# A hybrid mLSTM and gated-delta encoder block: smaller inversion chunks beside the products, and the next z job's first split moved ahead of the last pair's final step

## The chip, the cores and the metric

The kernel runs on one core of a Trainium2 chip. The metric is the device time of one execution in microseconds (us). Engines are named as in the profile: PE is TensorE (PEld its weight loads), DVE is VectorE, ACT is ScalarE, POOL is GpSimd, SP is SyncE. SPq, ACTq and POOLq are the DMA issues of these engines.

## The reference

One encoder layer on 256 tokens of width 2048, in float32. Cut to what matters here:

```python
h = rms_norm(x) * (1 + scale_m) + shift_m          # scale, shift, gate from silu(c) @ W_ada
proj = h @ w_in                                    # 18,512 columns, split into the branches
# branch A: bidirectional chunkwise mLSTM, 4 heads, q/k 256 wide, v and output gate 512 wide
# branch B: bidirectional gated delta rule, 16 heads of 128:
a_mat = I + beta * (k k^T) * decay_strict          # per chunk of 64 tokens, unit lower triangular
t_mat = triangular_solve(a_mat, I)                 # its inverse
u = t_mat @ (beta * v);  w = t_mat @ (beta * exp(g) * k)
# ... scan over the chunks; o_b = rms_norm(o) * silu(z)
x = x + gate_m * ((g_a * y_a + g_b * y_b) @ w_out)
x = x + gate_f * swiglu(rms_norm(x) * (1 + scale_f) + shift_f)
return rms_norm(x)
```

## The kernel before

Every large product is computed in three passes of 32-bit matmuls: the weights are loaded as float32 (`raw`), ACT writes their rounded high half (`wh`, L182 or L213), DVE subtracts it for the low half (`wl`, L184 or L215), and PE adds hi*hi, lo*hi and hi*lo (L187 to L189, L234 to L236). `raw`, `wh` and `wl` have three buffers each, shared by all jobs.

Two generators make the products. `fjob` makes 128 columns of `w_in` for all 256 tokens: two steps of one split and 24 matmuls of 256 columns. `tjob` makes 512 columns: eight steps of one split and twelve matmuls of 512 columns. One step of either is called a unit here. Such jobs, which nothing waits for soon, stand in the list `fills`: z of a group of delta-rule heads, v and the output gates of the mLSTM heads, the merge gates (`ma`, `mb`), and q and k of the mLSTM heads (`a`). `fill(n)` takes n units from the front of the list, and does nothing once the list is empty. The list is one fixed order, `[z0] + rest`, and each later z job is put at its front when its group comes up.

The delta rule goes in four groups `g` of four heads. A group's life is this:

- `gdn_phase1(h)` (two steps for each head) makes the decay matrices, the key products (`ks`) and the 32 by 32 diagonal blocks `mi`, which POOL writes to DRAM (`inst_d`) and reads back as `uu`. Its second step ends on DVE with the transpose of L657.
- `gdn_invert(g)` inverts the 64 blocks of a group at once, on DVE alone: 30 rounds of two operations (L704, L710) with i from 30 down to 1, on i times 31-i elements. A running size of the rounds stops it every so often (`yield`), and `invert(g)` issues one unit of products at each stop. Before the first round it issues four units (six for group 0). The result goes back to DRAM (`inv_d`).
- `gdn_blocks(g)` reads the blocks, transposes and spreads them; eight units and one unit are issued beside it.
- `gdn_phase2(g, p)` finishes the heads in two pairs p, in nine steps: `p1` to `p4` build the inverse of 128 by 128, `pa`, `pb`, `pc` apply it, `po` makes the output and starts its norm, and the ninth step transposes the normalised output (`px`, L841), copies it (`obt`, L845) and stores it to DRAM (`ob_d`).

Around the nine steps of a pair, `stream` hands out pieces: the products of the next two heads (`b` jobs) with their `gdn_phase1` steps, then units of `fills`. How many pieces follow each step stands in three tuples, for pair 0, pair 1 and group 3:

```python
    after = (0, 1, 2, 1, 2, 2, 2, 2, 4, 0)
    last = (0, 1, 2, 1, 2, 2, 1, 1, 3, 0)
    second = (0, 2, 2, 1, 2, 2, 2, 2, 3, 0)
```

For groups 0 to 2, the sixteenth and last piece of pair 1, behind step 8, carries the second `gdn_phase1` step of the last head of the next group. `heads[h]` are what that step leaves.

Behind group 3 the mLSTM heads 0 and 1 go on (`pden`, then `ph`), the pool `sx` of the delta rule is closed, the outputs of all groups are loaded (`o4`, L1076) and split (`obh` and `obl`, L1080 and L1081), and the products `yb` read them. `fill(1)`, `fill(2)` and `fill(1000)` stand in between and issue what is left of the list.

The program text is not the order on the engines. A planner (the tile framework's scheduler) orders each engine's instructions by when it expects them to be ready, and by their place in the text where several are. `order(ins)` restricts it: the instruction is kept behind the one issued just before it in the text on the same engine. In `tjob` it is used for the splits if `early` is not 0:

```python
            order(S.activation(wh, raws[u][:, k0 : k0 + 2], AF.Copy), early)
            settle()
            order(V.tensor_tensor(wl, raws[u][:, k0 : k0 + 2], wh.bitcast(F32), ALU.subtract), early)
```

`early` is also the number of splits that a job makes before its first matmul; the job then stops once. `settle()` issues what earlier steps have put off, among it the copies of the blocks' corners by ACT (L679, L682). A z job has `early=0` before, except the first (3). `pump()` in each unit moves on the sums of the modulation (`ada`, L124), which run beside the products.

Of the kernel before, what the change touches and what calls it, by code (L numbers as in the profile page):

```python
# [52 lines left out]
def hybrid_block(ctx: ExitStack, tc: tile.TileContext, xr, nfr, crow, pk_d, cst_d, ada2, ada4, win0, winb, wint, wba, wbb, wo, wgu, wd, out, dbg=None):  # L53
# [3 lines left out]
    def pool(stack, name, bufs=1, **kw):  # L57
        return stack.enter_context(tc.tile_pool(name=name, bufs=bufs, **kw))
# [13 lines left out]
    def order(ins, yes=True):  # L72

        return tc.keep_in_program_order(ins) if yes else ins
# [64 lines left out]
    def settle(keep=0, only=None):  # L139

        now = [f for f in behind if only is None or f.__name__ == only]
        for f in now[: len(now) - keep]:
            behind.remove(f)
            f()
# [122 lines left out]
    fills = []  # L267

    def fill(n=1):

        while n and fills:
            if next(fills[0], None):
                n -= 1
            else:
                fills.pop(0)
# [90 lines left out]
    def z_job(g, early=0):  # L366
        def done(ps):
            szs[g] = evp.tile([P, 2, 512], F32, tag="sz", bufs=1, name=f"sz{g}")
            for t in range(2):
                S.activation(szs[g][:, t], ps[t], AF.Silu)  # L370
        return tjob(f"z{g}", [wint[g, u] for u in range(4)], hh, hl, done, early)
# [121 lines left out]
    with ExitStack() as s0:  # L493
# [72 lines left out]
        zj = z_job(0, 3)  # L566
# [121 lines left out]
    def gdn_invert(g):  # L688

        uu = uus.pop(g)  # L690
        tmp = bk.tile([64, 256], F32, tag="utmp", bufs=1, name=f"utmp{g}")
        inv = inv_d[g].rearrange("j b (x h) i -> h (b x) j i", h=GRP)

        def store(rows):
            for e in range(GRP):
                G.dma_start(inv[e, :, rows], uu[16 * e : 16 * e + 16, rows])

        yield
        order(V.memset(uu.rearrange("p j i -> p (j i)")[:, ::33], 1.0))
        size = 0  # L700
        for i in range(30, 0, -1):
            w = 31 - i
            t3 = tmp[:, 0 : i * w].rearrange("p (j c) -> p j c", j=i)
            order(V.tensor_tensor(  # L704
                t3,
                uu[:, 0:i, i : i + 1].broadcast_to([64, i, w]),
                uu[:, i : i + 1, i + 1 :].broadcast_to([64, i, w]),
                ALU.mult,
            ))
            order(V.tensor_tensor(uu[:, 0:i, i + 1 :], uu[:, 0:i, i + 1 :], t3, ALU.add))  # L710
            if i == 16:
                store(slice(16, 32))
            size += i * w + 125
            if size > 720:
                size = 0
                yield
        store(slice(0, 16))

    def gdn_blocks(g):

        cg = bk.tile([P, 2, 512], F32, tag="uu", bufs=1, name=f"cg{g}")
        for b in range(4):
            G.dma_start(cg[32 * b : 32 * b + 32, 0], inv_d[g][:, b].rearrange("j x i -> j (x i)"))
        yield
        order(V.transpose(cg[:, 1], cg[:, 0]))
        F_, Bt, Ft, B_ = (cg[:, i // 2, (i % 2) * 256 : (i % 2 + 1) * 256].rearrange("p (m c) -> p m c", m=8) for i in range(4))

        def mix(dst, a, ca, b, cb):
            order(V.tensor_scalar(dst, b, cb, None, ALU.mult))
            order(V.scalar_tensor_tensor(dst, a, ca, dst, ALU.mult, ALU.add))  # L730

        mix(R[:, 0], Ft, even, Bt, odd)
        mix(R[:, 1], B_, even, F_, odd)
        yield
        for i, ab in enumerate(((Ft, Bt), (B_, F_))):
            for b in range(4):
                r = slice(32 * b, 32 * b + 32)
                order(S.activation(X[r, i, :, b % 2], ab[b // 2][r], AF.Copy))
            yield
        for i, a in enumerate((F_, B_)):  # L740
            for b in range(4):
                r = slice(32 * b, 32 * b + 32)
                if i:
                    order(V.tensor_copy(UL[r, i, :, r], a[r]))
                else:
                    order(S.activation(UL[r, i, :, r], a[r], AF.Copy))
            yield
# [139 lines left out]
    def stream(h0):  # L887

        todo = []

        def piece():

            for q in list(todo):
                q[0] -= 1
                if not q[0]:
                    todo.remove(q)
                    next(heads1[q[1]])

        for h in range(h0, min(h0 + 2, NH_B)):
            for j in range(3):  # L900
                for _ in b_job(h, j):
                    piece()
                    yield True
            todo += [[2, h], [4, h]]
        while todo:
            fill(1)
            piece()
            yield True
        while True:
            fill(1)  # L910
            yield True
# [106 lines left out]
    def invert(g):  # L1018
        gen = gdn_invert(g)
        next(gen)  # L1020
        fill(4 if g else 6)
        for _ in gen:
            fill(1)

    invert(0)
    for g in range(4):
        blocks = gdn_blocks(g)
        next(blocks)
        fill(8)
        next(blocks)  # L1030
        fill(1)
        pairs = [gdn_phase2(g, p) for p in range(2)]
        if g == 3:
            settle()
            sf.close()
            mq["pool"] = pool(sq_, "mq", side="right")
            first2 = [mlstm(h) for h in range(2)]
            for c in first2:
                next(c)
        every[0] = 1  # L1040
        for p in range(2):
            pieces = stream(4 * g + 2 * p + 4)
            for n in range(1, 10):

                held[0] = n < 4
                if p == 0:
                    next(blocks, None)
                next(pairs[p], None)
                if g == 3 and n == (8, 4)[p]:
                    next(first2[p])  # L1050
                for _ in range(last[n] if g == 3 else second[n] if p else after[n]):
                    next(pieces)
            for _ in pairs[p]:
                pass

            if g < 3:
                while 4 * g + 2 * p + 5 not in heads:
                    next(pieces)
        if g < 3:
            fills.insert(0, z_job(g + 1))  # L1060
            every[0] = owed[0] = 0
            invert(g + 1)
    settle()
# [499 lines left out]
```

## Time and profile before

| | us |
|---|---|
| median of 3 runs | 1973.03 (1969.95 to 1974.28) |
| the profiled execution | 1974.3 |
| its span, first to last instruction | 1972.4 |
| PE busy | 1929.4 |
| DVE busy | 1405.5 |
| ACT busy | 1030.0 |
| mean granted clock of PE | 0.994 |

The profile is of one execution. A row of a timeline gives the start, the duration, the engine, the line of the kernel, the operation, output and inputs by the program's names, and in brackets the idle time before it with what ended it. A row of a list of waits gives who waited for whom: total, number of times, longest. A row of a group gives count, busy time, mean ns of one, and idle time before. PE's matmuls are pipelined, so their durations overlap; the distance of two starts tells what one costs.

### The profile page before, as it was taken

To read this page: it belongs to the slowest core of one execution; us is meant where nothing else is said; L and a number is where in the kernel's file an instruction comes from. 1 tells how busy PE (TensorE), PEld (TensorE's weight loads), DVE (VectorE), ACT (ScalarE), POOL (GpSimd) and SP (SyncE) were. 2 spreads that over 40 slices of the span, in tenths; PEclk is the share of its full clock that TensorE was granted. 3 is DMA by queue.
4 is the path that set the end of the run, shared out by engine and by line. 5 is a ranking of instruction groups with operands and counts; after the bars stand their busy time and mean duration, and the time that the engine had idled before them with its cause. 6 is when DMAs were issued, how large, how long until landed. Compare 5 with 4: busy or idle time off the path is not lost.

```text
span 1972.4 us, 27079 instructions
## 1 busy us (share of the span) xinstructions
PE 1929.4 (98%) x10418; PEld 1703.5 (86%) x10418; DVE 1405.5 (71%) x2067; ACT 1030.0 (52%) x1555; POOL 116.5 (6%) x211
## 2 busy tenths in 40 slices
PE   8999999999999999999999999999999999999998
PEld 6878889998998899889787888888888888888886
DVE  6779887887888798866577878866665665555554
ACT  3137656764766577565544444644444444444444
POOL 0001210111001010110100000200000000000000
PEclk9999999999999999999999999999999999999999
DMA  9987676766566666586777888566676665565663
GB/s 399 420 349 226 184 249 240 252 214 208 203 217 213 237 218 229 192 296 246 277 282 266 323 317 330 191 252 238 238 265 241 237 238 205 197 213 197 208 199 142
DMA packets 78962, 485.64 MB, mean 246 GB/s; under 512 B 10585, under 2 KB 15969, under 8 KB 24433
## 3 DMA queue, kind: packets, MB, share of 16 engines
q1 hardware_dynamic: 63216, 450.69, 62.9%
q0 software_dynamic: 8160, 17.88, 4.5%
q10 hardware_dynamic: 7458, 15.36, 2.1%
q8 instruction: 81, 1.33, 0.3%
q14 instruction: 47, 0.39, 0.1%
HBM read 467.07 MB, written 16.82 MB: 245 GB/s over the span
## 4 chain that ended last, share of the span: by engine, by line
PE 81%; DVE 8%; DMA 6%; ACT 2%; issue 1%; POOL 0%; ACTq 0%; SPq 0%; DVEq 0%; POOLq 0%
PE acc_gt L234 4%; PE acc_gt L235 4%; PE acc_gt L236 4%; PE acc_up L236 4%; PE acc_up L235 4%; PE acc_up L234 4%; PE acc_d L236 4%; PE acc_d L235 4%; PE acc_d L234 4%; DMA ra<-ada 3%; PE acc_b L187 2%; PE acc_b L188 2%; PE acc_b L189 2%; PE acc_o L236 2%; PE acc_o L234 2%; PE acc_o L235 2%
## 5 line engine op out<-in xcount | busy, mean ns | idle before, releaser
L215 DVE TENSOR_TENSOR wl_d<-raw_d,wh_d 128x1024 fp32r<-128x1024 f32 x88 | 107.7, 1224 | 105.9 <-ACT wh_d L213 105.9
L215 DVE TENSOR_TENSOR wl_up<-raw_up,wh_up 128x1024 fp32r<-128x1024 f32 x88 | 107.7, 1224 | 100.2 <-ACT wh_up L213 100.1
L215 DVE TENSOR_TENSOR wl_gt<-raw_gt,wh_gt 128x1024 fp32r<-128x1024 f32 x88 | 108.1, 1229 | 80.2 <-ACT wh_gt L213 80.2
L187 PE MATMUL acc_b<-hh,wh_b 128*128 128x256 f32 x576 | 163.0, 283 | 0.6 <-ACT wh_b L182 0.6
L189 PE MATMUL acc_b<-hh,wl_b 128*128 128x256 f32 x576 | 159.6, 277 | 0.8 <-DVE wl_b L184 0.8
L188 PE MATMUL acc_b<-hl,wh_b 128*128 128x256 f32 x576 | 159.2, 276 | 0.0
L213 ACT ACTIVATE wh_d<-raw_d 128x1024 fp32r<-128x1024 f32 x88 | 92.9, 1056 | 126.5 <-PE acc_d L235 117.7
L213 ACT ACTIVATE wh_gt<-raw_gt 128x1024 fp32r<-128x1024 f32 x88 | 92.9, 1056 | 118.6 <-PE acc_gt L235 71.1
L213 ACT ACTIVATE wh_up<-raw_up 128x1024 fp32r<-128x1024 f32 x88 | 92.8, 1055 | 108.1 <-PE acc_up L235 77.1
L124 DVE SCALAR_TENSOR_TENSOR ada<-ada,crow 128x2048 f32<-128x2048 f32 x64 | 146.0, 2284 | 0.0
L234 PE MATMUL acc_gt<-wh_gt,hfh 128*128 128x512 f32 x352 | 135.6, 385 | 0.6 <-ACT hfh L1350 0.6
L235 PE MATMUL acc_gt<-wh_gt,hfl 128*128 128x512 f32 x352 | 134.9, 383 | 0.0
L236 PE MATMUL acc_gt<-wl_gt,hfh 128*128 128x512 f32 x352 | 134.1, 381 | 0.0
L234 PE MATMUL acc_up<-wh_up,hfh 128*128 128x512 f32 x352 | 133.4, 379 | 0.0
L235 PE MATMUL acc_up<-wh_up,hfl 128*128 128x512 f32 x352 | 133.4, 379 | 0.0
L236 PE MATMUL acc_up<-wl_up,hfh 128*128 128x512 f32 x352 | 133.4, 379 | 0.0
L234 PE MATMUL acc_d<-wh_d,ffh 128*128 128x512 f32 x344 | 130.5, 379 | 0.0
L235 PE MATMUL acc_d<-wh_d,ffl 128*128 128x512 f32 x344 | 130.5, 379 | 0.0
L236 PE MATMUL acc_d<-wl_d,ffh 128*128 128x512 f32 x344 | 130.4, 379 | 0.0
L561 PE MATMUL first<-x,raw 128*128 128x256 f32 x512 | 114.5, 382 | 7.2 <-ACT x L555 7.2
L561 PEld LDWEIGHTS first<-x,raw 128*128 128x128 f32 x512 | 96.0, 190 | 25.7 <-ACT x L555 13.3
L189 PEld LDWEIGHTS acc_b<-hh,wl_b 128*128 128x128 f32 x576 | 111.3, 193 | 1.0 <-DVE wl_b L184 1.0
(383 smaller groups left out, 5263.1 us busy)
## 6 DMA issues: line engine op xcount, KB each, us to landing
ada<-ada SPq DMA_DIRECT2D x64, 1024.0 KB, 6.0
raw_gt<-wgu SPq DMA_DIRECT2D x44, 1024.0 KB, 4.9
raw_up<-wgu SPq DMA_DIRECT2D x44, 1024.0 KB, 4.9
raw_d<-wd SPq DMA_DIRECT2D x44, 1024.0 KB, 4.9
raw_b<-winb SPq DMA_DIRECT2D x36, 1024.0 KB, 5.3
ra<-ada SPq DMA_DIRECT2D x32, 1025.0 KB, 15.8
raw<-win SPq DMA_DIRECT2D x16, 1024.0 KB, 14.5
raw_z<-wint SPq DMA_DIRECT2D x16, 1024.0 KB, 5.0
```

The lines of the kernel that those rows point to most:

```text
L124: order(V.scalar_tensor_tensor(raw, raw, 1.0, row_c[:, :D], ALU.mult, ALU.mult, accum_out=mod[:, c : c + 1]))
L187: PE.matmul(o, wh[:, k], woven(hh[:, kk]), start=kk == 0, stop=False)
L188: PE.matmul(o, wh[:, k], woven(hl[:, kk]), start=False, stop=False)
L189: PE.matmul(o, wl[:, k], woven(hh[:, kk]), start=False, stop=kk == KB - 1)
L213: order(S.activation(wh, raws[u][:, k0 : k0 + 2], AF.Copy), early)
L215: order(V.tensor_tensor(wl, raws[u][:, k0 : k0 + 2], wh.bitcast(F32), ALU.subtract), early)
L234: order(PE.matmul(ps[t], xh[:, kk, c], woven(wh[:, k]), start=kk == 0, stop=False), early and steps > 1)
L235: PE.matmul(ps[t], xl[:, kk, c], woven(wh[:, k]), start=False, stop=False)
L236: PE.matmul(ps[t], xh[:, kk, c], woven(wl[:, k]), start=False, stop=kk == last)
L561: PE.matmul(first[o], raw[:, o], x[:, b], start=b == 0 and o % 2 == 0, stop=b == KB - 1 and o % 2 == 1)
```

## The change

Two things. The limit at which `gdn_invert` stops goes from 720 to 580. And the z job of the next group is made with `early=1` and started at n = 9 of pair 1, ahead of the pair's ninth step; its remaining units go to the front of the list where the whole job went before.

```diff
@@ -711,7 +711,7 @@
                 store(slice(16, 32))
             size += i * w + 125
-            if size > 720:
+            if size > 580:
                 size = 0
                 yield
@@ -1045,6 +1045,9 @@
                 if p == 0:
                     next(blocks, None)
+                if g < 3 and p and n == 9:
+                    zj = z_job(g + 1, 1)
+                    next(zj)
                 next(pairs[p], None)
@@ -1057,7 +1060,7 @@
         if g < 3:
-            fills.insert(0, z_job(g + 1))
+            fills.insert(0, zj)
             every[0] = owed[0] = 0
             invert(g + 1)
```

## The prediction

> **What bounds the kernel now.** I read the page's totals first, then the chain that ended last, then who TensorE waited for, and only then the timelines around the places the diff touches.
>
> ```profile
> span 1972.4 us, 27079 instructions
> ...
> PE 1929.4 (98%) x10418; PEld 1703.5 (86%) x10418; DVE 1405.5 (71%) x2067; ACT 1030.0 (52%) x1555; POOL 116.5 (6%) x211
> ...
> PE 81%; DVE 8%; DMA 6%; ACT 2%; issue 1%; POOL 0%; ACTq 0%; SPq 0%; DVEq 0%; POOLq 0%
> ```
>
> TensorE (PE) is the bound over the whole span. The diff neither adds nor removes a matmul, so it can only move time in which PE stands still. The list of PE's waits has those that lie near the change:
>
> ```profile
> PE acc_z L234 <- ACT wh_z L213: 2.5, 1, 2.5
> PE acc_mb L236 <- DVE wl_mb L215: 1.8, 2, 1.0
> PE acc_ma L236 <- DVE wl_ma L215: 1.6, 2, 0.9
> PE acc_a L189 <- DVE wl_a L184: 0.2, 1, 0.2
> ```
>
> ```profile
> PE acc_mb L236 <- DVE wl_mb L215: 1.0, 1, 1.0
> PE acc_o L236 <- DVE wl_o L215: 0.8, 1, 0.8
> ```
>
> The second fence is the same list for the stretch from 435 to 480 us, the inversion of group 1. Each column is the total, the number of times and the longest. With one more pair in group 2 and a short one in group 3, PE loses 1.8 + 1.6 + 0.8 + 0.2 = 4.4 us to low splits (`wl`) that DVE delivers late, and 2.5 us where the z job of group 3 begins. These 6.9 us, with what the clock adds to the second (below), are the most that the change can win.
>
> **Part 1: smaller chunks.** VectorE (DVE) in the inversion stretch of group 1:
>
> ```profile
> L704 DVE TENSOR_TENSOR utmp<-uu 64x30 f32<-64x30 f32 (+14 forms) x30 | 9.7, 322 | 2.2 <-DMA uu<-inst_d 1.4
> L710 DVE TENSOR_TENSOR uu<-uu,utmp 64x30 f32<-64x30 f32 (+14 forms) x30 | 9.7, 322 | 0.8
> L215 DVE TENSOR_TENSOR wl_o<-raw_o,wh_o 128x1024 fp32r<-128x1024 f32 x7 | 8.5, 1209 | 0.0
> ```
>
> One inversion is 60 operations of 322 ns, 19.3 us, and one low split is 1.21 us. The loop's own size sums to 8,710 over the 30 rounds; at a limit of 720 it stops 10 times, at 580 it stops 12 times (and one round is left for after the last stop). At each stop `fill(1)` issues one unit of products: one split and twelve 512-column matmuls (or 24 of 256 columns), which PE starts 0.215 us apart:
>
> ```profile
> 429.88 0.38 PE L235 MATMUL acc_z<-wh_z,hl 128*128 128x512 f32 x1
> 430.09 0.38 PE L236 MATMUL acc_z<-wl_z,hh 128*128 128x512 f32 x1
> 430.31 0.38 PE L234 MATMUL acc_z<-wh_z,hh 128*128 128x512 f32 x1
> ```
>
> So a unit is 12 x 0.215 = 2.58 us of PE. The largest chunk now (rounds 20 to 18, size 1,057) is 1,057 / 8,710 x 19.3 = 2.34 us, and with its split 3.55 us: PE falls 0.97 us behind, which is the size of the waits above. After the change the largest (823) gives 1.82 + 1.21 = 3.03 us and the usual one (712) 1.58 + 1.21 = 2.79 us, still a little over 2.58 but without the jumps. By itself this part wins at most the 4.4 us, and at least nothing.
>
> It also takes 2 units more in each of four inversions, 8 units or 20.6 us of PE work, from a list with an end. I count the list: z jobs 4 x 8, the four v jobs 32, the merge, gate and k/q jobs 26 + 3 x 32: 186 units. Now 19 go in the gates, 18 in the first four heads, 6 + 10 + 3 x (4 + 10) = 58 in the inversions, 36 at the blocks, 24 in the pairs of groups 0 to 2 and 26 in those of group 3: 181, and the five that remain stand in the `fill(1)`, `fill(2)` and `fill(1000)` behind the last pair. With 66 in the inversions the list is empty three calls before the end of the last pair, and those eight calls issue nothing. What they issue now is in PE's groups from the end of `po` of the last pair (938.6) to the first matmul of `yb` (972.6):
>
> ```profile
> L234 PE MATMUL acc_ma<-wh_ma,hh 128*128 128x512 f32 x32 | 12.8, 399 | 0.0
> L235 PE MATMUL acc_ma<-wh_ma,hl 128*128 128x512 f32 x32 | 12.1, 379 | 0.0
> L236 PE MATMUL acc_ma<-wl_ma,hh 128*128 128x512 f32 x32 | 12.1, 379 | 0.0
> L978 PE MATMUL ph<-vt,mdec 128*128 128x512 f32 x24 | 10.5, 592 | 0.0
> L962 PE MATMUL pden<-ones,mdec 128*128 128x1 f32 x24 | 2.7, 247 | 0.0
> L841 PE MATMUL px<-cst,on 128*128 128x128 f32 x4 | 0.6, 272 | 0.0
> ```
>
> 96 `acc_ma` matmuls are exactly eight units. Without them 10.5 + 2.7 + 0.6 = 13.8 us of PE work are left to cover the way from `po` to `yb`. That way is a chain:
>
> ```profile
> 938.22 0.39 PE L834 MATMUL po<-z,at 128*128 128x128 f32 x2
> ```
>
> ```profile
> 941.84 1.13 DVE L868 SCALAR_TENSOR_TENSOR on<-po,so,sz 128x128 f32<-128x128 f32 x4
> ```
>
> ```profile
> 947.17 0.82 ACT L845 ACTIVATE obt<-px,pk 128x256 f32<-128x256 f32 x2
> ...
> 958.72 1.06 ACT L1080 ACTIVATE obh<-o 128x1024 fp32r<-128x1024 f32 x1 [3.16 <-DMA o<-ob_d]
> ```
>
> ```profile
> 951.18 1.51 POOL L1076 DMA_DIRECT2D o<-ob_d  x2 [57.51 <-ACT dn L964]
> ```
>
> ```profile
> 959.81 1.22 DVE L1081 TENSOR_TENSOR obl<-o,obh 128x1024 fp32r<-128x1024 f32 x1 [2.99 <-ACT obh L1080]
> ```
>
> `po` ends at 938.61 and the normalised heads are ready at 942.97, 4.4 us later. The transposes (0.6 us) could follow; now they sit behind three units. From the start of `obt` (947.17) over its store, the release of the group's pool (all of `sx`, so POOL issues the `o` loads only at 951.18), the load and the split, `obl` is there at 961.03: 13.9 us. With no units in between `obt` starts at about 942.97 + 0.6 + 0.35 = 943.9 (0.35 is my estimate for the step from PE to ACT) and `obl` stands at 957.8, that is 19.2 us behind the end of `po`. PE then idles 19.2 - 13.8 = 5.4 us. Lower bound: 2.4 us, if the load, which takes 7.5 us here, lands 3 us sooner in a quieter moment. Upper bound: 10.6 us, if the second half of `ph` (about 5.2 us) also waits, because its PSUM banks are drained by ACT, whose queue would then hold `obh` ahead. I take 5.4.
>
> **Part 2: the z job ahead.** With `early=1` every split of this job goes through `order`, which pins it behind the instruction issued before it on its engine. That matters more than the place of the call. At n = 9 the last thing issued on DVE is the second step of the pair's last head, ending in the transpose of L657. Today z's low splits are free and the planner puts them well ahead of it:
>
> ```profile
> 424.53 1.22 DVE L215 TENSOR_TENSOR wl_z<-raw_z,wh_z 128x1024 fp32r<-128x1024 f32 x1
> ...
> 431.27 0.43 DVE L657 STREAM_TRANSPOSE mi<-mb 128x256 f32<-128x256 f32 x1
> ...
> 438.50 1.23 DVE L215 TENSOR_TENSOR wl_z<-raw_z,wh_z 128x1024 fp32r<-128x1024 f32 x1 [1.22 <-ACT wh_z L213]
> 441.15 0.19 DVE L704 TENSOR_TENSOR utmp<-uu 64x30 f32<-64x30 f32 x1 [1.42 <-DMA uu<-inst_d]
> ```
>
> Pinned, the first `wl_z` of group 1 starts at 431.70 and ends at 432.9, and the first L236 moves from 430.09 to there: 2.8 us of PE. Nothing else is in reach: `ks` and `px` are done, and later units need the same three split buffers. Group 2 has the same picture:
>
> ```profile
> 613.50 0.38 PE L236 MATMUL acc_z<-wl_z,hh 128*128 128x512 f32 x1
> ```
>
> ```profile
> 614.68 0.43 DVE L657 STREAM_TRANSPOSE mi<-mb 128x256 f32<-128x256 f32 x1
> ```
>
> 615.11 + 1.2 = 616.3 against 613.50, again 2.8 us. The pins also hold z's fifth split behind the first chunk, its sixth behind the second, and so on, while today six are done (the first and the last of them stand above) when the inversion starts (at 441.15, when `uu` lands, which the change doesn't move). For the first 16 units of group 1 (4 ahead, 12 at the stops) DVE then needs until 441.15 + 19.3 - 0.3 + 12 x 1.21 = 474.7, and PE ends 2.58 us later, at 477.2; now PE begins z at 429.6, two matmuls ahead of that L236, and the same 16 end at 429.6 + 16 x 2.58 + 1.8 = 472.7. So +4.5 us if DVE sets the pace throughout, +1.0 (2.8 less the 1.8 of part 1) if the later, unpinned splits slip ahead of the chunks as they do now. DVE is full there, so I take the upper half: 3.5 us each for groups 1 and 2, in which part 1's gain is already spent.
>
> Group 3 is the place where the step helps:
>
> ```profile
> 790.30 0.60 PE L841 MATMUL px<-cst,on 128*128 128x128 f32 x4
> 793.41 0.79 PE L234 MATMUL acc_z<-wh_z,hh 128*128 128x512 f32 x1 [2.51 <-ACT wh_z L213]
> ...
> 794.67 0.79 PE L236 MATMUL acc_z<-wl_z,hh 128*128 128x512 f32 x1
> ```
>
> ```profile
> 792.36 0.43 DVE L657 STREAM_TRANSPOSE mi<-mb 128x256 f32<-128x256 f32 x1
> 793.39 1.23 DVE L215 TENSOR_TENSOR wl_z<-raw_z,wh_z 128x1024 fp32r<-128x1024 f32 x1 [0.60 <-ACT wh_z L213]
> ```
>
> The high split can move ahead of `obt`, but the low one still stands behind L657: 792.79 + 1.23 = 794.02 instead of 794.62. I take -0.6 us; if both came in time it would be -2.5 us and what the clock costs. The moved call issues one load on SP, one ACT and one DVE instruction; the load was issued early before, POOL gets nothing new, and the two `obt` copies behind the ACT split are read only by their store.
>
> After this wait PE runs slow for a while; the row is that of the windows, PEclk behind the five busy times:
>
> ```profile
> 793.28:796.69 3.41, 3.24 (x7) 2.15 (x8) 1.86 (x2) 3.33 (x9) 1.97 (x4) 0.50 0.11 19
> ```
>
> Half the clock for 3.41 us costs 1.7 us, and a wait of 2.5 us was enough. I add 1.7 us once, for the idle time of 5.4 us at the end of group 3, and none for the waits of 2.8 us in groups 1 and 2, where DVE sets the pace behind them; 3.4 us for those two go into the upper bound. The Trainium skill, "TensorE: Matmul & The Clock Gate", Part 1, says that the clock is halved after at least one idle window of about 3.4 us, free-running: by that rule the 2.8 us waits would cost no clock at all, and the 3.4 us would leave my upper bound; the row, where 2.5 us sufficed, speaks against relying on it.
>
> **Sum.** +3.5 +3.5 -0.6 +5.4 +1.7 = +13.5 us. The profiled execution took 1974.3 us (span 1972.4 and 1.9 around it) and would become 1987.8; the median of the three runs is 1.3 us lower, so 1973.0 + 13.5 = 1986.5. One `ada` step fewer is done before group 3 ends and returns in the `o` products, where DVE is ahead of PE; I cost it at nothing, and at 2.3 us (one `ada` operation) if it isn't hidden.
>
> **Rivals.** *Faster.* The point that decides is whether the planner still gets z's first low split out before PE needs it (an earlier `ks`, hence an earlier L657) and whether the end of group 3 is cheap. For it: the planner already brings z's splits forward in groups 1 and 2. Against it: L657 hangs on `ks`, which PE runs just before `px`. If both hold: -4.4 - 2.5 - 1.7 + 2.4 = -6.2 us, 1966.8. *Even:* the waits go (-8.6) and the end costs its 5.4 + 1.7: -1.5 us, 1971.5; with one of the two handovers late it is +1.3, 1974.3. *The end is covered:* the planner draws `pden` and `ph` so far forward that only the handovers count: 3.5 + 3.5 - 0.6 + 1 = +7.4, 1980.4. *Worse:* `ph` stalls behind `obh` and both handovers pay for the clock: 13.5 + 5.2 + 3.4 = +22.1, 1995.1.
>
> **How the numbers follow.** 0.2% (3.9 us) is about what a measurement of this kernel can tell from no change. Forecast 0.50 (its own range 1982 to 1992), covered end 0.17, worse 0.10, even 0.11, faster 0.12. The first three are all slower by over 0.2%: 0.77. The even case gives 0.10 for within 0.2% and its rest goes to faster: 0.13. The range leaves out the faster case and the top of the worse one: 1973 to 1994.
>
> **What would show it.** Of the changed kernel: the waits of `acc_z` L236 on `wl_z` in groups 1 and 2, near 2.8 us each, and the first `wl_z` right behind L657 in all three handovers; twelve stops in the inversions and no wait of 0.9 us in their middle; no `acc_ma` matmul between the last `po` and `yb`, and PE idle there for 5 us, with the clock at 0.50 behind it. I am wrong if `wl_z` still stands ahead of L657, or if PE finds other products behind the last `po`.

## The result, and the profile after

| | before | after |
|---|---|---|
| median, us | 1972.8 (1968.5 to 1974.4, 6 runs) | 1986.93 (1984.4 to 1990.8, 6 runs) |
| ratio | | 1.0077, 95% interval 1.0060 to 1.0094 |
| span of the profiled execution, us | 1972.4 | 1986.4 |

The changed kernel is 14.1 us slower by the medians and 15.2 us by the ratio (the ratio is of means); the forecast was 1986.5. The page after, totals and chain:

```profile
span 1986.4 us, 27089 instructions
...
PE 1935.6 (97%) x10418; PEld 1709.4 (86%) x10418; DVE 1405.3 (71%) x2067; ACT 1025.5 (52%) x1551; POOL 116.9 (6%) x211
...
PE 83%; DVE 6%; DMA 6%; ACT 2%; issue 2%; POOL 0%; SPq 0%; ACTq 0%; DVEq 0%; POOLq 0%
```

PE still sets the time, with as many matmuls (10418). PE's list of waits over the whole span (total, times, longest):

```profile
PE acc_z L236 <- DVE wl_z L215: 14.1, 7, 4.9
PE first L561 <- ACT x L555: 6.9, 15, 1.7
PE px L841 <- DVE on L868: 3.6, 1, 3.6
...
PE acc_o L236 <- DVE wl_o L215: 2.4, 2, 2.1
...
PE p L770 <- DVE pt L762: 1.2, 1, 1.2
```

The waits for the low splits of `ma` and `mb`, the 0.9 us ones in the middle of the inversions, are gone, and the one wait for z's high split too. In their place PE waits 14.1 us for z's low split. In group 2's handover the timelines of PE and DVE show how:

```profile
622.38 0.60 PE L841 MATMUL px<-cst,on 128*128 128x128 f32 x4
...
623.47 0.38 PE L235 MATMUL acc_z<-wh_z,hl 128*128 128x512 f32 x1
626.02 1.12 PE L236 MATMUL acc_z<-wl_z,hh 128*128 128x512 f32 x2 [2.18 <-DVE wl_z L215]
```

```profile
624.43 0.43 DVE L657 STREAM_TRANSPOSE mi<-mb 128x256 f32<-128x256 f32 x1
624.79 1.18 DVE L215 TENSOR_TENSOR wl_z<-raw_z,wh_z 128x1024 fp32r<-128x1024 f32 x1
```

The first low split stands right behind L657, as the pin demands. From the L235 at 623.47 to the L236 at 626.02 are 2.55 us where 0.215 would do: 2.34 us lost, and the same 2.34 us in groups 1 and 3. The waits of PE that the text names are taken in this way, from start to start; they come out some 0.16 us longer than the idle time in the lists.

The clock behind the waits, in the view of stretches (the first number behind the five busy times is the granted clock):

```profile
439.90:443.30 3.40, 3.19 (x15) 2.82 (x16) 3.40 (x6) 2.84 (x3) 1.67 (x4) 1.00 0.30 46
626.16:629.57 3.41, 3.41 (x9) 2.66 (x10) 3.41 (x5) 1.70 (x3) 2.19 (x4) 0.50 0.33 43
643.23:646.64 3.41, 3.41 (x10) 2.69 (x9) 3.20 (x9) 0.00 (x0) 0.00 (x0) 0.50 0.00 0
820.72:824.13 3.41, 3.41 (x9) 2.69 (x10) 2.36 (x2) 1.74 (x3) 1.14 (x3) 0.50 0.36 58
380.40:383.81 3.41, 3.41 (x18) 3.41 (x17) 3.41 (x7) 2.23 (x8) 1.67 (x4) 0.50 0.48 130
970.91:981.15 10.24, 8.60 (x32) 6.97 (x33) 2.09 (x13) 2.55 (x7) 1.35 (x2) 0.50 0.15 46
```

Of three equal waits of 2.34 us two were followed by 3.41 us at half clock (rows 2 and 4), the one in group 1 was not (row 1). Row 3 lies behind a longer wait inside group 2's inversion, row 5 behind a wait of 1.34 us of `p` for `pt` in group 0 (1.2 in the list). The last row is the end of group 3, whose PE groups from the last `po` to `yb` are:

```profile
L978 PE MATMUL ph<-vt,mdec 128*128 128x512 f32 x24 | 12.0, 661 | 0.0
L962 PE MATMUL pden<-ones,mdec 128*128 128x1 f32 x24 | 5.1, 334 | 0.0
L841 PE MATMUL px<-cst,on 128*128 128x128 f32 x4 | 1.6, 462 | 3.6 <-DVE on L868 3.6
L234 PE MATMUL acc_yb<-wh_yb,obh 128*128 128x512 f32 x1 | 0.8, 780 | 0.0
```

No `acc_ma` is left there; PE stands for 3.6 us until the norm (`on`) is ready, and of the 17.1 us from there to `yb` (972.55 to 989.67) it spends 8.6 at half clock.

**Where the time went.** From the starts of all PE instructions I take, for each stage, the time beyond 0.2155 us for a 512-column matmul and 0.108 us for a narrower one, and subtract the same of the kernel before. "z1" is the first matmul of z of group 1, "p1" the first of a group's `p1`. Half clock counts in it. us, one profile each:

| stage | after | e1 | e2 | e3 | e5 | e6 | e7 | e8 | e9 | e10 | e12 |
|---|---|---|---|---|---|---|---|---|---|---|---|
| p1 g0 to z1 | 3.1 | 4.6 | 0.0 | 3.1 | 1.5 | 2.9 | 0.0 | 0.0 | 1.5 | 4.6 | 0.0 |
| z1 to p1 g1 | 2.1 | -0.4 | 2.9 | -1.0 | 1.9 | 2.0 | 2.5 | 0.1 | 2.2 | -0.9 | 0.1 |
| p1 g1 to z2 | -4.7 | -4.7 | -4.7 | -4.6 | -4.8 | -4.8 | -4.5 | -0.1 | -4.8 | -4.6 | -4.6 |
| z2 to p1 g2 | 8.7 | 0.2 | 7.3 | 4.6 | 6.0 | 7.3 | 7.9 | 3.8 | 3.9 | 1.9 | 0.0 |
| p1 g2 to z3 | -0.2 | -1.9 | -2.0 | -1.9 | -1.9 | -1.9 | -1.5 | -2.0 | -1.9 | -1.9 | -3.3 |
| z3 to p1 g3 | 1.8 | -1.3 | 4.8 | -1.7 | 4.7 | 1.5 | 3.9 | 2.4 | 4.4 | -2.0 | 1.7 |
| last po to yb | 7.5 | 6.8 | 0.0 | 6.8 | 7.9 | 6.8 | 1.9 | 1.7 | 7.6 | 8.5 | 2.2 |
| ya to gate | -3.0 | -3.3 | 0.2 | -3.3 | -3.1 | -3.0 | 0.2 | -1.6 | -0.8 | -3.3 | -0.8 |

The columns e1 to e12 are the experiments below (e4 is near e1). A repeat of the kernel before, e11, moved one stage of the table by 1.7 us and the others by 0.5 us or less, so differences under 2 us between single profiles say little. A piece of half clock is 1.7 us, and it need not come back at the same place: the 1.7 us of e11 are such a piece (762.03), and the changed kernel's -0.2 between p1 of group 2 and z3, where most others have -1.9, holds one too (786.59).

The 3.1 us of group 0 are the wait of 1.34 us for `pt` with the half clock behind it. The wait is there in every kernel that has taken two units more by then (the changed one, e1, e3, e4, e5, e6, e9, e10) and in none of the others.

### The profile page after: what moved, and what is told of

Its sections match the earlier page's. It is cut to its first block, busy times and chain, and to the rows that moved or that the text cites. A ratio compares the mean times of both kernels' runs of the same rounds, so it can differ in the third digit from the quotient of the medians.

```text
span 1986.4 us, 27089 instructions
## 1 busy us (share of the span) xinstructions
PE 1935.6 (97%) x10418; PEld 1709.4 (86%) x10418; DVE 1405.3 (71%) x2067; ACT 1025.5 (52%) x1551; POOL 116.9 (6%) x211
## 4 chain that ended last, share of the span: by engine, by line
PE 83%; DVE 6%; DMA 6%; ACT 2%; issue 2%; POOL 0%; SPq 0%; ACTq 0%; DVEq 0%; POOLq 0%
PE acc_gt L234 4%; PE acc_gt L235 4%; PE acc_gt L236 4%; PE acc_up L236 4%; PE acc_up L235 4%; PE acc_up L234 4%; PE acc_d L235 4%; PE acc_d L236 4%; PE acc_d L234 4%; DMA ra<-ada 3%; PE acc_o L236 2%; PE acc_b L187 2%; PE acc_o L234 2%; PE acc_o L235 2%; PE acc_b L189 2%; PE acc_b L188 2%
## 5 line engine op out<-in xcount | busy, mean ns | idle before, releaser
L235 PE MATMUL acc_gt<-wh_gt,hfl 128*128 128x512 f32 x352 | 135.0, 384 | 0.0
L236 PE MATMUL acc_gt<-wl_gt,hfh 128*128 128x512 f32 x352 | 134.2, 381 | 0.0
L235 PE MATMUL acc_up<-wh_up,hfl 128*128 128x512 f32 x352 | 133.4, 379 | 0.0
L236 PE MATMUL acc_up<-wl_up,hfh 128*128 128x512 f32 x352 | 133.4, 379 | 0.0
L235 PE MATMUL acc_d<-wh_d,ffl 128*128 128x512 f32 x344 | 130.5, 379 | 0.0
L236 PE MATMUL acc_d<-wl_d,ffh 128*128 128x512 f32 x344 | 130.4, 379 | 0.0
```

Source lines behind the costliest of these rows:

```text
L235: PE.matmul(ps[t], xl[:, kk, c], woven(wh[:, k]), start=False, stop=False)
L236: PE.matmul(ps[t], xh[:, kk, c], woven(wl[:, k]), start=False, stop=kk == last)
```

## The experiments

Each ratio is against the kernel before, run beside it; the us given with it are what the ratio makes of that kernel's median.

**e1, e2: one part each.** e1 is the kernel before with the smaller chunks, e2 the changed kernel with the old limit.

```diff
# e1, on the kernel before
-            if size > 720:
+            if size > 580:
# e2, on the changed kernel
-            if size > 580:
+            if size > 720:
```

> The limit 580 with the z jobs as before (no early call, no pins). Theory A (two costs: the list of units runs out at the end of group 3, and the pins of the z splits): the waits inside the inversions go (-4.4 us) and the end of group 3 costs what it did in the changed kernel (about +7 us): +2 to +4 us against the kernel before, near 1976; the profile shows no acc_ma between the last po and yb, and the first wl_z ahead of L657 in groups 1 and 2. Rival B (the pins are the whole loss, the end is covered): -4 us, near 1969. Rival C (the list is the whole loss): the full +14 us, near 1987.

> The z job called early with its pins, the limit at 720. Theory A: the list lasts, so no cost at the end of group 3; a wait of about 2.3 us of acc_z L236 at each of the three handovers (in group 3 in place of the 2.5 us of before), and with chunks of the old size and no splits ahead further waits inside the inversions of groups 1 to 3: +5 to +11 us, near 1981. Rival B (pins are the whole loss): +14 us or more. Rival C (the list is the whole loss): within 1 us of the kernel before or 2 us faster.

Measured: e1 0.9988 (0.9979 to 0.9997), -2.4 us; e2 1.0037 (1.0024 to 1.0050), +7.3 us. The smaller chunks, to which the prediction gave the loss at the end of group 3, gain a little: less than B's 4 us, and not A's loss of 2 to 4. The end is no less open in e1 (+6.8 us), as A said; it is paid for by other stages. e2 lies in A's bounds. And -2.4 + 7.3 = 4.9 us is far from the 15.2 us that 1.0077 makes of 1973: the parts are not additive. The table shows one reason. Both parts, each alone, bring -4.7 us between p1 of group 1 and z2 and -2 us between p1 of group 2 and z3; together they bring the first once and the second hardly. PE's waits in the stretch from p1 of group 1 to z2, first in the kernel before, then in the changed one:

```profile
PE vps L609 <- ACT vf L341: 1.4, 1, 1.4
PE p L770 <- DVE pt L762: 1.0, 1, 1.0
PE acc_b L189 <- DVE wl_b L184: 0.8, 1, 0.8
PE acc_b L187 <- ACT wh_b L182: 0.6, 1, 0.6
```

```profile
PE vps L609 <- ACT vf L341: 1.5, 1, 1.5
PE pb L819 <- DVE r L820: 0.3, 1, 0.3
```

Before, PE comes to `p1` while the first `b` splits and `pt` are not done. Whatever makes PE come some us later, two units more in the inversion or a wait for a pinned split, takes these waits away. Some 3 of the 4.7 us are these waits; the rest is a piece of half clock that the kernel before has in this stretch and the changed one has not:

```profile
581.65:585.07 3.42, 3.42 (x18) 3.42 (x17) 2.37 (x8) 2.25 (x5) 0.00 (x0) 0.50 1.01 417
```

**e3: the pins.** The changed kernel, but in the z jobs of groups 1 to 3 the splits are not pinned.

```diff
-            order(S.activation(wh, raws[u][:, k0 : k0 + 2], AF.Copy), early)
+            order(S.activation(wh, raws[u][:, k0 : k0 + 2], AF.Copy), early and pin)
...
-            order(V.tensor_tensor(wl, ...), early)
+            order(V.tensor_tensor(wl, ...), early and pin)
...
-        return tjob(f"z{g}", ..., done, early)
+        return tjob(f"z{g}", ..., done, early, pin=not g)
```

> The changed kernel, but the splits of the z jobs of groups 1 to 3 are not pinned (no order around them); the early call stays. Theory A: the first wl_z stands ahead of L657 again, no wait at the handovers, also not in group 3 (-4.2 us with the clock), no waits in the inversions (-4.4 us), the end of group 3 as in the changed kernel (+7 us): -1.5 us against the kernel before, near 1971.5, 15 us better than the changed kernel. Rival C (the list is the whole loss): near 1984. Rival D (the early call itself, its load and its ACT split, does the harm): near 1987.

**e4: the list.** The kernel before with ten units beside the blocks, which empties the list as early as the smaller chunks do.

```diff
-        fill(8)
+        fill(10)
```

> The kernel before with fill(10) in place of fill(8) beside the blocks of each group: the eight units are taken earlier, in another place, and nothing else changes (limit 720, z jobs as before). Theory A: only the end of group 3 pays, PE idle for 7 to 8 us between the last po and yb, clock at half behind it: +5 to +8 us, near 1980. Rival B (pins are the whole loss): within 1 us of the kernel before.

Measured: e3 1.0004 (0.9995 to 1.0013), +0.8 us; e4 0.9990 (0.9981 to 0.9999), -2.0 us. Against the changed kernel's 1.0077 the pins cost 0.73%, 14 us. Against e1, which has the same chunks, the early call without pins costs some 3 us, with intervals that just overlap. And e4, which changes nothing but where the units go, reproduces e1: +8.1 us at the end of group 3, +3.0 in group 0, -4.8, -1.9 and -3.1 us elsewhere. Neither theory had a gain for it. So the hole behind the last `po` is real in place and size, and an empty list is still no loss of its own.

**e5, e6: which pin.** e5 pins only the first split of those z jobs, e6 all but the first.

```diff
+            order(..., early and pin in (None, u + k0 > 0))
# e5: pin=False for groups 1 to 3; e6: pin=True; z of group 0 keeps all its pins (None)
```

> Both parts of the change, but of the z jobs of groups 1 to 3 only the first split is pinned; the other seven are free. On DVE the first low split then stands right behind L657, as in the changed kernel, and five or six splits stand ahead of the inversion. Theory A, the wait at the handover is the loss (2.34 us in each of three, and the half clock it may set off): close to the changed kernel, 10 to 14 us over the kernel before. Theory B, the pins inside the inversion are the loss (fifth and later splits behind the chunks, PE dry while uu is on its way): the three handover waits of about 2.3 us stay, the waits near 637 us go, and the total is 4 to 8 us over the kernel before. Theory C, the two overlap (DVE sets the pace, so a wait at the handover is made up later): within 3 us of the kernel before.

> The counterpart: the first split of the z jobs of groups 1 to 3 is free, the other seven are pinned. On DVE the first low split stands ahead of L657 in all three groups, the second behind L657, and four splits ahead of the inversion as in the changed kernel. Theory A: no handover wait of 2.3 us, total within 3 us of the kernel before. Theory B: no handover wait, but the pinned waits inside the inversions stay (5 us in group 2), so 5 to 9 us over the kernel before. Theory C: the first unit merely starts earlier and PE waits for the second or the fifth split instead, so 8 to 14 us over.

Measured: e5 1.0066 (1.0053 to 1.0079), +13.0 us; e6 1.0058 (1.0042 to 1.0074), +11.4 us. PE's waits in group 2 from the handover on, e5 and then e6:

```profile
PE acc_z L236 <- DVE wl_z L215: 5.4, 2, 3.2
PE acc_mb L236 <- DVE wl_mb L215: 0.3, 1, 0.3
```

```profile
PE acc_z L236 <- DVE wl_z L215: 5.0, 1, 5.0
PE acc_z L234 <- ACT wh_z L213: 1.1, 1, 1.1
```

e5 keeps the handover waits, 2.34 us three times as theory A says, and its total falls into A's bounds; yet A's counterpart fails, for e6 without them is hardly faster. (The second wait of e5's first row is not a handover: `uu` of group 2 landed late there too, 12.38 us behind L657, see e9.) e6 begins its first unit early, then waits for the second split (1.3 us each time) and the fifth (1.9, 5.1 and 1.4 us), which is theory C. Either set of pins alone costs nearly what both cost. A reading that fits, and that no run tests further, is that PE needs splits at a steady pace and one pinned link is enough to hold it.

**e7, e8: a list that lasts.** The changed kernel (e7) and e3 (e8) with `fill(6)` beside the blocks instead of `fill(8)`.

> The changed kernel with six units beside the blocks instead of eight, so that the list of products lasts behind the last pair as it did before. If the end of group 3 is a loss of its own (7.5 us of idle there in the changed kernel), this is 5 to 8 us faster than the changed kernel, that is 6 to 9 us over the kernel before. If what is lost there was won elsewhere by the same shift (as the two kernels with the list run out and no pins suggest, which were 2.4 and 2.7 us under the kernel before), it is within 3 us of the changed kernel, 12 to 16 us over the kernel before, with acc_ma matmuls again between the last po and yb and waits again between the inversion and z of the next group or in ya.

> Limit 580, the z job made ahead with no split of groups 1 to 3 pinned, and six units beside the blocks, so that the list lasts. If the end of group 3 costs 6.8 us net and nothing is given up for it, this is 5 to 7 us under the kernel before. If the units taken earlier are what removes waits elsewhere, it is within 3 us of the kernel before, with idle time back before z of group 2 and in ya.

Measured: e7 1.0055 (1.0042 to 1.0067), +10.9 us; e8 1.0022 (1.0012 to 1.0032), +4.3 us. With pins the longer list helps by some 4 us, less than the 5.6 us that it saves at the end of group 3, and with intervals that overlap; without pins it is a loss of 3.5 us against e3. Both medians miss what was expected: e7 falls between its two cases (6 to 9 and 12 to 16 us over the kernel before), and e8 is a little slower than either of its two. e8's waits between p1 of group 1 and z2 are those of the kernel before again, as expected:

```profile
PE vps L609 <- ACT vf L341: 1.4, 1, 1.4
PE p L770 <- DVE pt L762: 1.0, 1, 1.0
PE acc_b L189 <- DVE wl_b L184: 0.8, 1, 0.8
```

**e9, e10: the 5 us in group 2.** Even without pins (e3) the z job ahead costs group 2 4.6 us, while groups 1 and 3 gain. The timelines of POOL, SP and DVE in group 2, kernel before:

```profile
616.54 2.18 POOL L663 DMA_DIRECT2D inst_d<-mi  x4 [13.94 <-DVE wl_z L215]
620.52 0.51 POOL L670 DMA_DIRECT2D uu<-inst_d  x1 [1.80 <-DMA inst_d<-mi]
```

```profile
618.70 0.33 SPq L210 DMA_DIRECT2D raw_z<-wint  x1
```

```profile
624.52 0.20 DVE L704 TENSOR_TENSOR utmp<-uu 64x30 f32<-64x30 f32 x1 [1.39 <-DMA uu<-inst_d]
```

The same three in the changed kernel:

```profile
626.29 2.19 POOL L663 DMA_DIRECT2D inst_d<-mi  x4 [12.74 <-DVE wl_z L215]
632.98 0.52 POOL L670 DMA_DIRECT2D uu<-inst_d  x1 [4.50 <-DMA inst_d<-mi]
```

```profile
628.03 3.95 SPq L210 DMA_DIRECT2D raw_z<-wint  x2
```

```profile
639.54 0.19 DVE L704 TENSOR_TENSOR utmp<-uu 64x30 f32<-64x30 f32 x1 [7.58 <-issue]
```

Counted from the end of L657 (615.11 and 624.86), the fourth small write of `inst_d` is issued at 3.06 us in both. The 1 MB load of z's weights follows at 3.59 us before, and the write lands 1.72 us after its issue; at 3.17 us after the change, and the write takes 4.43 us. So POOL waits 4.50 us instead of 1.80 and issues `uu` at 8.12 us instead of 5.41, behind a second such load (6.79 us); `uu` lands at 14.56 us, 0.18 us after that load, instead of 9.29. The inversion starts 5 us late, and the fifth z split, pinned behind its first chunk, with it. That is the 4.9 us wait, by DVE and by PE:

```profile
641.52 1.21 DVE L215 TENSOR_TENSOR wl_z<-raw_z,wh_z 128x1024 fp32r<-128x1024 f32 x1
```

```profile
642.79 0.48 PE L236 MATMUL acc_z<-wl_z,hh 128*128 128x512 f32 x1 [4.89 <-DVE wl_z L215]
```

In e3 the write takes 4.41 us in the same way, and the planner puts the fifth split behind the first chunk though no pin asks for it (the chunk begins at 634.93, the split at 636.61): a wait of 2.99 us. e9 and e10 hold the load back behind a later low split, in group 2 alone: z's third chunk on the changed kernel (e9), z's fourth on e3 (e10).

```diff
+            if name == "z2" and (u, k0) == (1, 0):        # e10: (2, 0), and 3 for 2 below
+                raws[2] = raw_tile([P, 4, 512], f"raw_{name}_2")
+                order(V.memset(raws[2][:, 0, 0:1], 0.0))
+                nc.sync.dma_start(raws[2], chunks[2])
             return wh, wl
```

> The changed kernel, and in group 2 the load of z's third chunk of weights is held back behind the third low split, by a one-column write into its buffer, so that it is issued about 1 us later (4.2 us behind the end of L657 instead of 3.17). If that load's packets are what made the last small write of inst_d take 4.4 us instead of 1.7 and the read of uu be issued at 8.1 us instead of 5.4 (and land at 14.6 us), then in group 2 the write lands by 5 us, uu is issued near 5.4 and lands near 10 us, the wait of 5.05 us in the inversion of group 2 falls to 1 us or less, and the total is 4 to 6 us under the changed kernel, that is 8 to 10 us over the kernel before. If uu is late for another reason (the pins, the place of its issue on POOL), uu still lands 12 us or more behind L657 and the total stays 12 to 15 us over the kernel before.

> The kernel without pins on the z jobs of groups 1 to 3 (limit 580, z made ahead), and in group 2 the load of z's fourth chunk, the one that is issued at 3.17 us behind L657 there, is held back behind the fifth low split, to about 4.5 us. If the meeting of this load with the small writes is why making the z job ahead costs group 2 its 4.4 us even without pins, uu lands near 10 us behind L657 instead of 13.9, the wait of 2.99 us goes, and the total is 3 to 4.5 us under that kernel, that is 2.5 to 4.5 us under the kernel before. If not, it stays within 1.5 us of the kernel before.

POOL, SP and DVE of e9 (its lines lie 4 further down; L657's transpose ends at 623.73):

```profile
625.15 2.18 POOL L667 DMA_DIRECT2D inst_d<-mi  x4 [13.36 <-DVE wl_z L215]
629.13 0.52 POOL L674 DMA_DIRECT2D uu<-inst_d  x1 [1.80 <-DMA inst_d<-mi]
```

```profile
628.09 0.33 SPq L219 DMA_DIRECT2D raw_z<-wint  x1
```

```profile
634.65 0.19 DVE L708 TENSOR_TENSOR utmp<-uu 64x30 f32<-64x30 f32 x1 [3.14 <-issue]
```

With the load 1.2 us later the write takes 1.72 us again, POOL's wait is 1.80 again, `uu` is issued at 5.41 and lands at 10.80 us, and the wait inside group 2's inversion falls from 5.05 us to 1.29, start to start. So what the load does to the write in group 2 is shown, and the other profiles agree there: with the load issued 0.03 to 0.12 us behind the fourth write (e2, e3, e6, e7, e8) it took 4.29 to 4.94 us, with 0.5 us or more between them (e1, e4, e11, e12) 1.72 to 2.56. The distance alone is not the rule: in group 1 of e5 a load 0.35 us behind left the write at 1.73 us, and in group 3 of the changed kernel one 1.18 us behind went with 3.12. The price of the collision in the total is not settled: e9 measured 1.0062 (1.0043 to 1.0081), +12.2 us, 3 us under the changed kernel where 4 to 6 were expected, and the intervals overlap; its group 3 happened to wait 2.47 us for a `uu` that landed 10.25 instead of 8.55 us behind L657. e10 measured 0.9997 (0.9987 to 1.0006), 1.4 us under e3, with intervals that overlap, where 3 to 4.5 were expected: the load went out at 5.53 us instead of 4.5, half a us ahead of `uu` (6.02), which landed at 11.12 (13.85 in e3) just behind it. The wait fell only from 2.99 to 2.25 us.

**e11: the kernel before once more.**

> The kernel before once more, for its profile alone. If the waits that stood only in its first profile (0.73, 0.94 and 1.12 us between p1 of group 1 and z of group 2, with 3.4 us of half clock; 2.32 and 1.82 us in ya) belong to the kernel, they stand here too, at the same places, with a span within 2 us of 1972.4. If they were chance, the span is 5 us shorter or the idle time lies elsewhere.

Span 1975.3 us. Every wait named stands again at its place: 0.76, 0.94 and 1.12 us behind p1 of group 1 and 2.32 and 1.82 us in ya. So does the half clock behind them (581.12). They belong to the kernel. The span is 2.9 us longer, where at most 2 were expected: 1.7 us of half clock ahead of z3 (762.03) and small pieces.

**e12: the list handed out by stage.** The chunks alone (e1), with units given back where they hurt.

```diff
-        fill(8)
+        fill(8 if g in (1, 2) else 6)
...
-                for _ in range(last[n] if g == 3 else ...):
+                for _ in range(0 if (g, p, n) == (3, 1, 8) else last[n] if g == 3 else ...):
```

> The smaller chunks alone (limit 580, the z job as before), with the list of products handed out otherwise: six units instead of eight beside the blocks of groups 0 and 3, and none behind step 8 of the last pair, so that about four units are left behind the last po. If the stages add up: the 4.6 us between p1 and z in group 0 goes (it was set off by the list's shift), the shift's gains in groups 1 and 2 stay (4.7 and 1.9 us), the end of group 3 falls from 6.8 us over the kernel before to about 2, and ya may give its 3.3 us back; 5 to 8 us under the chunks alone, that is 6 to 10 us under the kernel before (0.995 to 0.997). If the waits only move with the list, as they did from the end of group 3 to other places, it stays within 3 us of the kernel before.

Measured: 1969.19 us against 1975.85 beside it, 0.9972 (0.9959 to 0.9984), -5.5 us: faster than both kernels. PE's groups from the last `po` to `yb`:

```profile
L978 PE MATMUL ph<-vt,mdec 128*128 128x512 f32 x24 | 10.7, 596 | 1.7 <-ACT hs L980 1.7
L234 PE MATMUL acc_ma<-wh_ma,hh 128*128 128x512 f32 x16 | 6.6, 414 | 0.0
```

Four units (48 matmuls, 16 on each of three lines) are enough to cover the chain: the stage costs 2.2 us more than before instead of 6.8, and the 4.6 us of group 0 are gone. 2.5 us of ya's 3.3 came back and z3 cost 3.0 more than in e1, so it came out just short of the 6 to 10 us expected. Against e1 it is some 3 us by the ratios, where 5 to 8 were expected.

## Why the prediction was right, and where it was not

The direction, the size and the two places were right; the division between them was not. That the number came out within half a us is luck: two errors of some 6 us cancelled.

- **The handovers: place right, size half.** The first `wl_z` stands right behind L657 in all three, and the wait is 2.34 us for 2.8: PE first ran four matmuls that need only the high split, where the working had two (0.43 us). For groups 1, 2 and 3 the sum had +3.5, +3.5 and -0.6 = 6.4 us; from z to p1 they measured +2.1, +8.7 and +1.8, with -0.2 ahead of z3: 12.4 us. The step that failed is "when `uu` lands, which the change doesn't move": it was read in group 1, where it held (9.28 us behind L657 before, 8.85 after), and carried over to group 2, where `uu` landed 5.3 us later because the moved job's load met the small writes. Of the two half clocks (1.7 us each) that the prediction kept for its upper bound, the one of group 2 came and the one of group 1 didn't; another came behind the wait inside group 2's inversion. In group 3 the wait itself went as worked out: 2.34 us for the low split in place of 2.67 for the high one (-0.3 us for -0.6), with half clock behind it in both kernels. Of that group's +1.6, 1.7 us are half clock ahead of z3 (786.59), which nothing here ties to the change.
- **The end of group 3: right, by another division.** From the end of `po` to `yb` 20.8 us were measured (968.91 to 989.67); the working had 19.2, and with 1.7 for the clock 20.9. PE stands at `px` (3.6 us), not ahead of `yb` (5.4), and the half clock costs up to 4.3 us instead of 1.7 (half of the 8.60 us that PE was busy in its 10.24). The term was 7.1 us, the stage shows 7.5.
- **What the sum left out.** The eight units that leave the end make PE later at other places, and there waits vanish: from the table -4.7 and -3.0, against +3.1 in group 0, with the small ones -5.9 us. The prediction counted the units as lost cover and gave nothing for their new place. The pins would have brought the -4.7 by themselves, for e2 has it with a list that lasts; the -3.0 is there in e1 (-3.3) and not in e2 (+0.2). So 6.4 + 7.1 stood for 12.4 + 7.5 - 5.9 = 14.0.
- **By cause** the runs say that the smaller chunks alone gain 2.4 us, that the early call added to them costs 3.2, and that the pins added to both cost 14.4; together 15.2. The rival "the end is covered" named the handovers as the whole loss; its number, +7.4, was low for the changed kernel and near e2's +7.3, where the list lasts. Its reason (the end costs nothing) does not hold in its place and holds in the sum.
- **The clock.** The Trainium skill, "TensorE: Matmul & The Clock Gate", Part 1, has the clock halved after at least one idle window of about 3.4 us; by it the handover waits would have cost no clock. The trace does not agree: 2.34 us sufficed in two of three. Without these two pieces the changed kernel would have come out 3.4 us lower, and the kernel before 1.7 us, for its wait of 2.5 us at 793.28.

What stays open: the net price of the collision in group 2. By stages it is 2.7 us (e10 against e3) to 4.8 us (e9 against the changed kernel); the totals do not resolve it.

## What to carry to other kernels

A pin on an early step holds it behind everything issued before it, so look first at what that is: here the planner had already moved the step ahead, and the pin took it back. When work is taken from a list that covers a later hole, cost its new place too: the stage that loses the cover shows the loss, the gain is spread over stages where PE now arrives later than its operands. Two edits that both delay the same arrival collect the same gain once, so test them apart and together.

## What the runs showed of the hardware

- A 16 KB write and a 64 KB read were held up by a 1 MB load on another queue. With 0.1 us between the issues of the fourth write and of the load, in group 2, the write took 4.43 us instead of 1.72 (0.53 us apart); other groups show that the distance alone doesn't decide. `uu`, issued behind such a load, landed 0.2 to 0.6 us after that load did in groups 1 and 2 of both kernels (in group 2, 9.29 us behind L657 after 9.09, and 14.56 after 14.38). The Trainium skill, "DMA: Bandwidth & Descriptors", Queues, rings and completion order, says that each DMA engine takes turns between queues only at the boundary of a packet, typically of some 9 to 17 descriptors. A load of 128 rows of 8 KB would give each of 16 engines 8 descriptors (an estimate from the load's shape and that page); if these went as one packet, a small transfer behind it would wait for all of it. The landings of `uu` agree with that. The fourth write doesn't: the sixteen 1 KB pieces of its data ran from 631.24 to 631.65, in the middle of the load's 128 pieces of 8 KB, of which 76 had begun before. Why the write waited as long as it did stays open.
- Half clock came in pieces of 3.41 us, once three in a row (10.24 us), after waits of 2.34 us (twice of three times) and after one of 1.34 us (380.40), which was preceded by narrow matmuls. Over the five kernels with such handovers (the changed one, e2, e5, e7, e9) a wait of 2.34 us came 13 times, and half clock began within 1.1 us of its end in 6 of them: the length of the wait alone does not decide.
